# Batched transposed matmul: b as bf16 pairs four rows to a partition, next batch's transposes ahead

## Chip, cores, metric

The kernel runs on one core of one Trainium2 chip. The metric is the device time of one execution in microseconds (us), median of several; the profile's own span is 1.7 to 1.9 us shorter than that time.

Names: PE is TensorE, which multiplies and also transposes; PEld is its loading of weights; DVE is VectorE, ACT ScalarE, POOL GpSimd, and SP the queue that issues the DMAs. PSUM is the memory that PE writes to; an eviction is a copy out of it. A transfer has landed when all 16 DMA engines have done their part of it. LAG n means that the output of a batch is stored n batches later. The granted clock is a share of TensorE's full clock.

## The reference

```python
batch, m, k, n = 16, 512, 512, 512
a: (batch, k, m) float32      b: (batch, n, k) float32
out = np.matmul(a.transpose(0, 2, 1), b.transpose(0, 2, 1))     # (batch, m, n) float32
```

Each batch reads 1 MiB of a and 1 MiB of b and writes 1 MiB: 48 transfers, 50.33 MB in all. b has k along its rows, so it must be transposed on the chip before it can be multiplied.

## The kernel before

```python
a_v = a.rearrange("b (ki ko) m -> b ki ko m", ko=KO)     # partition = 4 rows in a run: 8 KB
b_v = b.rearrange("b (no ni) k -> b ni no k", ni=P)      # partition = 4 rows 128 apart: 4 x 2 KB
out_v = out.rearrange("b (mi mo) n -> b mi mo n", mo=MO) # 8 KB
...                      # pools: a and b 3 buffers, o 8; PSUM 4 + 4 banks
LAG = 6                                                  # outputs are stored six batches later
for i in range(B):
    ...                                                  # load b, load a (both on the SP queue)
    for rk in range(KO):
        nc.scalar.copy(a_bf[:, rk, :], a_sb[:, rk, :])               # L60: a to bf16
    for rk in range(KO):
        bt_ps = psum_t.tile([P, N], f32)
        for no in range(NO):                                         # L68: 16 fp32 transposes
            nc.tensor.transpose(bt_ps[:, no * P:(no + 1) * P], b_sr[:, no, rk, :], identity)
        nc.vector.tensor_copy(bt_sb[:, rk, :], bt_ps)                # L73: to bf16
    for rm in range(MO):
        ...                                                          # L80: 4 matmuls into o_ps
        if rm % 2 == 0: nc.scalar.copy(o_sb[:, rm, :], o_ps)         # L88
        else:           nc.vector.tensor_copy(o_sb[:, rm, :], o_ps)  # L90
    if i >= LAG: emit_out_dma(i - LAG)
for j in range(B - LAG, B): emit_out_dma(j)
```

## Time and profile before

| | before |
|---|---|
| time | 129.46 us (129.3 to 129.65) |
| span in the profile | 127.8 us |
| DMA queue 1 | 97.5% of 16 engines' span, 13056 packets |
| PE / DVE / ACT busy | 72% / 48% / 43% |

The first lines are from the page of the kernel before: the span in 40 equal slices (DMA busy in tenths, then GB/s), the packets, the DMA queue, and the chain of work that ended last.

```profile
DMA  3999999999999999999999999999999999999980
GB/s 90 402 370 422 406 399 420 382 409 398 404 417 415 417 419 394 416 410 429 420 410 423 406 436 405 416 426 413 427 402 431 412 424 418 426 428 428 426 346 36
DMA packets 13063, 50.42 MB, mean 394 GB/s; under 512 B 768, under 2 KB 768, under 8 KB 8960
...
q1 hardware_dynamic: 13056, 50.33, 97.5%
...
DMA 50%; PE 34%; SPq 3%; ACT 1%; issue 1%; DVE 1%; ACTq 0%
```

The DMA engines are busy in every slice but the first and the last two. The 8960 packets under 8 KB are b's 8192 packets of 2 KB and 768 small ones that signal completion; a and out are 4096 packets of 8 KB. The rate rises from about 400 to 420 GB/s as outputs mix in and holds 426 to 428 in the last full slices, which move outputs alone. That fits slower packets of b, but the row alone doesn't show it: loads of a and b are mixed in it.

The groups of instructions (busy us, mean ns of one | idle before, and what ended it), and the waits (us in total, times, longest):

```profile
L80 PE MATMUL o_ps<-bt_sb,a_bf 128*128 128x512 bf16 x248 | 59.0, 385 | 9.1 <-ACT a_bf L60 8.7
L73 DVE CAST bt_sb<-bt_ps 128x512 bf16<-128x512 f32 x64 | 40.0, 683 | 14.7 <-PE bt_ps L68 14.7
L68 PE MATMUL bt_ps<-identity,b_sb 128*128 128x128 f32 x256 | 35.7, 295 | 12.8 <-DMA b_sb<-in_b_dram 12.8
```

```profile
ACT a_bf L60 <- DMA a_sb<-in_a_dram: 39.5, 13, 6.8
```

ACT, which casts a, waits 39.5 us for a's transfers. The compute engines wait for the DMA, not the DMA for them.

The end of the span, by window: PE, PEld, DVE, ACT, POOL busy us (instructions), granted clock, DMA share, GB/s.

```profile
110.00:115.00 5.00, 3.64 (x15) 1.61 (x16) 2.12 (x4) 3.35 (x6) 0.00 (x0) 1.00 1.01 424
115.00:120.00 5.00, 0.00 (x0) 0.00 (x0) 0.10 (x1) 0.00 (x0) 0.00 (x0) 0.74 1.02 431
120.00:123.00 3.00, 0.00 (x0) 0.00 (x0) 0.00 (x0) 0.00 (x0) 0.00 (x0) 0.50 1.01 429
123.00:126.00 3.00, 0.00 (x0) 0.00 (x0) 0.00 (x0) 0.00 (x0) 0.00 (x0) 0.50 0.40 169
```

Compute is over at 115.1 us and the DMA goes on at its full rate to about 123 us: seven outputs were still to be stored when the last load came in.

### The profile page before, as it was taken

The numbers are of one execution on the slowest core, as the hardware profiler recorded it, in microseconds if no ns is written. First come the engines' busy times: TensorE is split into PE (matmuls) and PEld (weight loads), VectorE is DVE, ScalarE is ACT, GpSimd is POOL, SyncE is SP. The second block draws the span as 40 slices with busy tenths as digits, with TensorE's granted clock in tenths as the row PEclk, the third lists the DMA queues.
The fourth block names the chain that finished last, engine by engine and source line by source line (L and its number), as shares of the span: only waits on it lengthen the run. The fifth ranks groups of instructions, "written<-read, shape, count | busy, mean of one in ns | idle before, by whom it ended". The sixth has DMA issues, their size and how long they took to land.

```text
span 127.8 us, 1405 instructions
## 1 busy us (share of the span) xinstructions
PE 92.5 (72%) x504; PEld 60.6 (47%) x512; DVE 61.5 (48%) x96; ACT 54.8 (43%) x97; POOL 0.7 (1%) x6
## 2 busy tenths in 40 slices
PE   0099999999999995768767796877779777670000
PEld 0094858678586763364634536353364634430000
DVE  0053668586774865463544727355472635640000
ACT  4026747646674635407163460816337072540000
POOL 2000000000000000000000000000000000000000
PEclk9999999999999999999999999999999999998555
DMA  3999999999999999999999999999999999999980
GB/s 90 402 370 422 406 399 420 382 409 398 404 417 415 417 419 394 416 410 429 420 410 423 406 436 405 416 426 413 427 402 431 412 424 418 426 428 428 426 346 36
DMA packets 13063, 50.42 MB, mean 394 GB/s; under 512 B 768, under 2 KB 768, under 8 KB 8960
## 3 DMA queue, kind: packets, MB, share of 16 engines
q1 hardware_dynamic: 13056, 50.33, 97.5%
q8 instruction: 4, 0.07, 0.2%
q14 instruction: 3, 0.02, 0.0%
HBM read 33.55 MB, written 16.78 MB: 394 GB/s over the span
## 4 chain that ended last, share of the span: by engine, by line
DMA 50%; PE 34%; SPq 3%; ACT 1%; issue 1%; DVE 1%; ACTq 0%
DMA a_sb<-in_a_dram 32%; PE o_ps L80 22%; DMA out_dram<-o_sb 13%; PE bt_ps L68 12%; DMA b_sb<-in_b_dram 4%; SPq L56 3%; ACT a_bf L60 1%; DVE o_sb L90 1%; ACT o_sb L88 0%; ACTq L60 0%; SPq L50 0%
## 5 line engine op out<-in xcount | busy, mean ns | idle before, releaser
L80 PE MATMUL o_ps<-bt_sb,a_bf 128*128 128x512 bf16 x248 | 59.0, 385 | 9.1 <-ACT a_bf L60 8.7
L60 ACT CAST a_bf<-a_sb 128x512 bf16<-128x512 f32 x64 | 34.9, 615 | 39.6 <-DMA a_sb<-in_a_dram 39.5
L73 DVE CAST bt_sb<-bt_ps 128x512 bf16<-128x512 f32 x64 | 40.0, 683 | 14.7 <-PE bt_ps L68 14.7
L68 PE MATMUL bt_ps<-identity,b_sb 128*128 128x128 f32 x256 | 35.7, 295 | 12.8 <-DMA b_sb<-in_b_dram 12.8
L80 PEld LDWEIGHTS <-a_bf 128*128 128x128 bf16 x256 | 27.3, 115 | 35.8 <-ACT a_bf L60 17.7
L68 PEld LDWEIGHTS bt_ps<-identity,b_sb 128*128 128x128 f32 x256 | 33.9, 211 | 17.5 <-PE o_ps L80 8.5
L90 DVE COPY o_sb<-o_ps 128x512 f32<-128x512 f32 x32 | 22.1, 692 | 38.9 <-PE o_ps L80 21.9
L88 ACT COPY o_sb<-o_ps 128x512 f32<-128x512 f32 x32 | 18.8, 586 | 19.0 <-PE o_ps L80 18.9
L60 ACT ACT_TABLE_LOAD x1 | 1.3, 1283 | 0.7 <-PEq L111 0.7
masks.py:199 POOL TENSOR_SCALAR_AFFINE_SELECT identity<-identity 128x128 f32<-128x128 f32 x1 | 0.3, 292 | 0.1
masks.py:197 POOL MEMSET identity<- 128x128 f32 x1 | 0.2, 204 | 0.3 <-POOLq L111 0.3
L111 POOL MEMSET const-bfloat16-1.0<- 128x1 bf16 x1 | 0.1, 101 | 0.0
L111 POOL MEMSET const-uint8-127<- 128x1 uint8 x1 | 0.1, 101 | 0.0
L111 POOL MEMSET const-float32-0.0<- 128x1 f32 x1 | 0.1, 98 | 0.2 <-issue 0.2
L111 POOL MEMSET const-float32-1.0<- 128x1 f32 x1 | 0.1, 98 | 0.0
## 6 DMA issues: line engine op xcount, KB each, us to landing
b_sb<-in_b_dram SPq DMA_DIRECT2D x16, 1024.0 KB, 15.4
a_sb<-in_a_dram SPq DMA_DIRECT2D x16, 1024.0 KB, 17.3
out_dram<-o_sb SPq DMA_DIRECT2D x16, 1024.0 KB, 17.4
```

What stands on the lines that cost most here:

```text
L56: nc.sync.dma_start(a_sb, a_v[i])
L60: nc.scalar.copy(a_bf[:, rk, :], a_sb[:, rk, :])
L68: nc.tensor.transpose(bt_ps[:, no * P:(no + 1) * P], b_sr[:, no, rk, :], identity,)
L73: nc.vector.tensor_copy(bt_sb[:, rk, :], bt_ps)
L80: nc.tensor.matmul(o_ps, a_br[:, rk, rm, :], bt_sb[:, rk, :], start=(rk == 0), stop=(rk == KO - 1),)
L88: nc.scalar.copy(o_sb[:, rm, :], o_ps)
L90: nc.vector.tensor_copy(o_sb[:, rm, :], o_ps)
L111: nc = _bacc.Bacc("TRN2", target_bir_lowering=False, num_devices=1)
```

## The change

Four rows of b in a run go to one partition, so that b too moves in 8 KB packets; the copy out of PSUM then puts n back in order. b is cast to bf16 first and transposed as 32-bit words of two bf16 values, which halves the transposes; the matmuls read every second bf16 of the result. And the source puts the transposes of batch i ahead of the matmuls of batch i-1. Besides, outputs lag by three batches in place of six, and the buffers of a and b go from three to four.

```diff
-    b_v = b.rearrange("b (no ni) k -> b ni no k", ni=P)
+    b_v = b.rearrange("b (ni no) k -> b ni no k", no=NO)
 ...  (a_pool, b_pool 3 -> 4; ac_pool 4 -> 3; bc_pool 2 new; o_pool 8 -> 6)
-    LAG = 6
+    LAG = 3
 ...
+    def prepare(i):
+        bc = bc_pool.tile([P, NO, K], cdt, name="bc")
+        nc.vector.tensor_copy(bc, b_sb)                                  # L65
+        bc_w = bc.bitcast(f32).rearrange("p no (pk j) -> p no j pk", j=KJ)
+        bt_w = bt_sb.rearrange("p j (ni no) -> p j ni no", no=NO)
+        for j in range(KJ):
             for no in range(NO):
-                nc.tensor.transpose(bt_ps[:, no * P:(no + 1) * P], b_sr[:, no, rk, :], identity)
-            nc.vector.tensor_copy(bt_sb[:, rk, :], bt_ps)
+                nc.tensor.transpose(bt_ps[:, no, :], bc_w[:, no, j, :], identity)           # L74
+            nc.vector.tensor_copy(bt_w[:, j, :, :], bt_ps.rearrange("p no ni -> p ni no"))  # L75
+        b_use[i] = bt_sb.bitcast(cdt).rearrange("p j (n h) -> p j h n", h=2)
 ...  (a is cast in two copies of 1024 columns: L80; matmuls L89; output copies L97 ACT, L99 DVE)
+    for i in range(B + 1):
+        if i < B:
+            load(i); prepare(i)
+        if i >= 1:
+            multiply(i - 1)
+        if i >= LAG + 1:
+            nc.sync.dma_start(out_v[i - 1 - LAG], o_tiles.pop(i - 1 - LAG))
```

More of the change, by code (lines that the diff above doesn't have):

```diff
@@ L23 @@
     KO = K // P
+    KJ = KO // 2
     MO = M // P
@@ L36 @@
     make_identity(nc, identity)
-    a_pool = ctx.enter_context(tc.tile_pool(name="a_pool", bufs=3))
-    b_pool = ctx.enter_context(tc.tile_pool(name="b_pool", bufs=3))
-    ac_pool = ctx.enter_context(tc.tile_pool(name="ac_pool", bufs=4))
+    a_pool = ctx.enter_context(tc.tile_pool(name="a_pool", bufs=4))
+    b_pool = ctx.enter_context(tc.tile_pool(name="b_pool", bufs=4))
+    ac_pool = ctx.enter_context(tc.tile_pool(name="ac_pool", bufs=3))
+    bc_pool = ctx.enter_context(tc.tile_pool(name="bc_pool", bufs=2))
@@ L41 @@
     bt_pool = ctx.enter_context(tc.tile_pool(name="bt_pool", bufs=3))
-    o_pool = ctx.enter_context(tc.tile_pool(name="o_pool", bufs=8))
+    o_pool = ctx.enter_context(tc.tile_pool(name="o_pool", bufs=6))
     psum_t = ctx.enter_context(tc.tile_pool(name="psum_t", bufs=4, space=bass.MemoryType.PSUM))
     psum_o = ctx.enter_context(tc.tile_pool(name="psum_o", bufs=4, space=bass.MemoryType.PSUM))
-    LAG = 6
-    o_tiles = {}
-    def emit_out_dma(j):
-        nc.sync.dma_start(out_v[j], o_tiles.pop(j))
@@ L52, with load @@
-    for i in range(B):
-        b_sb = b_pool.tile([P, NO, K], f32)
+    LAG = 3
+    o_tiles, a_tiles, b_tiles, a_use, b_use = {}, {}, {}, {}, {}
+    def load(i):
+        b_tiles[i] = b_sb = b_pool.tile([P, NO, K], f32, name="b_sb")
         nc.sync.dma_start(b_sb, b_v[i])
-        a_sb = a_pool.tile([P, KO, M], f32)
+        a_tiles[i] = a_sb = a_pool.tile([P, KO, M], f32, name="a_sb")
         nc.sync.dma_start(a_sb, a_v[i])
-        a_bf = ac_pool.tile([P, KO, M], cdt)
-        for rk in range(KO):
-            nc.scalar.copy(a_bf[:, rk, :], a_sb[:, rk, :])
-        a_br = a_bf.rearrange("p rk (pm rm) -> p rk rm pm", rm=MO)
-        b_sr = b_sb.rearrange("p no (pk rk) -> p no rk pk", rk=KO)
-        bt_sb = bt_pool.tile([P, KO, N], cdt)
-        for rk in range(KO):
-            bt_ps = psum_t.tile([P, N], f32)
-            for no in range(NO):
-                nc.tensor.transpose(
-                    bt_ps[:, no * P:(no + 1) * P],
-                    b_sr[:, no, rk, :],
-                    identity,
-                )
-            nc.vector.tensor_copy(bt_sb[:, rk, :], bt_ps)
-        o_sb = o_pool.tile([P, MO, N], f32)
-        o_tiles[i] = o_sb
+    def prepare(i):
+        b_sb, a_sb = b_tiles.pop(i), a_tiles.pop(i)
+        bc = bc_pool.tile([P, NO, K], cdt, name="bc")
+        nc.vector.tensor_copy(bc, b_sb)
+        bc_w = bc.bitcast(f32).rearrange("p no (pk j) -> p no j pk", j=KJ)
+        bt_sb = bt_pool.tile([P, KJ, N], f32, name="bt_sb")
+        bt_w = bt_sb.rearrange("p j (ni no) -> p j ni no", no=NO)
+        for j in range(KJ):
+            bt_ps = psum_t.tile([P, NO, P], f32, name="bt_ps")
+            for no in range(NO):
+                nc.tensor.transpose(bt_ps[:, no, :], bc_w[:, no, j, :], identity)
+            nc.vector.tensor_copy(bt_w[:, j, :, :], bt_ps.rearrange("p no ni -> p ni no"))
+        b_use[i] = bt_sb.bitcast(cdt).rearrange("p j (n h) -> p j h n", h=2)
+        a_bf = ac_pool.tile([P, KO, M], cdt, name="a_bf")
+        for h in range(2):
+            nc.scalar.copy(a_bf[:, 2 * h:2 * h + 2, :], a_sb[:, 2 * h:2 * h + 2, :])
+        a_use[i] = a_bf.rearrange("p rk (pm rm) -> p rk rm pm", rm=MO)
@@ L77, with multiply @@
+    def multiply(i):
+        a_br, bt_h = a_use.pop(i), b_use.pop(i)
+        o_tiles[i] = o_sb = o_pool.tile([P, MO, N], f32, name="o_sb")
         for rm in range(MO):
-            o_ps = psum_o.tile([P, N], f32)
+            o_ps = psum_o.tile([P, N], f32, name="o_ps")
             for rk in range(KO):
@@ L82 @@
                     a_br[:, rk, rm, :],
-                    bt_sb[:, rk, :],
+                    bt_h[:, rk // 2, rk % 2, :],
                     start=(rk == 0),
@@ L90 @@
                 nc.vector.tensor_copy(o_sb[:, rm, :], o_ps)
-        if i >= LAG:
-            emit_out_dma(i - LAG)
+    for i in range(B + 1):
+        if i < B:
+            load(i)
+            prepare(i)
+        if i >= 1:
+            multiply(i - 1)
+        if i >= LAG + 1:
+            nc.sync.dma_start(out_v[i - 1 - LAG], o_tiles.pop(i - 1 - LAG))
     for j in range(B - LAG, B):
-        emit_out_dma(j)
+        nc.sync.dma_start(out_v[j], o_tiles.pop(j))
 _INS = ['a', 'b']
```

## The prediction

> **What bounds the kernel now.** The DMA engines. Queue 1 takes 97.5% of 16 engines' span (page, DMA queues), and the slices show DMA at 9 from about 3 to 122 us. It moves 50.33 MB; the issue-by-issue record keeps about 16 engines occupied from 2.8 to 122.8 us. The windows give 404-412 GB/s while only loads run (20-40 us), 416-424 once outputs mix in, 431 when only outputs remain (115-120 us). PE is 9.95 of 10 us busy only until about 45 us (5.37 us a batch); afterwards PE, DVE and ACT wait for loads (ACT for a_sb 39.5 us, PE for b_sb 12.8 us, view of waits). The chain of waits is 50% DMA.
>
> **What the change does to compute (off the critical path).** Per batch: 16 transposes become 8 (about 120 ns apart in the chain of waits: -0.96 us PE); four 0.68 us bt evictions become two fp32 ones (-1.4 us DVE), plus one DVE cast of 2048 columns. Estimate for that cast: at the rate of the 683 ns eviction it would be at most 2.3 us, probably about 1.2 from SBUF at double rate. ACT casts 4x615 ns become two of about 1.05 us (estimate). Matmuls (about 215 ns apart) now read b at a 4-byte step; the Trainium skill, "SBUF - State Buffer", section "Door 1: The DMA port swizzle", calls up to 8 bf16 of step free; no run here shows it for the moving operand yet. PE then needs about 4.4 us a batch, DVE 4-5, ACT 3.3, against 7.4 us of DMA. All this only moves waits; PE stops bounding the first 45 us, but the DMA engines had no gap there either, so that is worth nearly nothing.
>
> **What matters: b's packets.** b is read today as 8192 packets of 2 KB, a and out as 4096 of 8 KB. With four rows to a partition b also becomes 2048 packets of 8 KB. The packet records have 84 ns median (86 mean) per 2 KB and 309 (313) per 8 KB: 4x84 = 336 against 309. Packets overlap, so I fitted packets to wall time: 80-83 ns per 2 KB, 307-313 per 8 KB, or 320-332 against about 309 per 8 KB. Saving: 2048 x 11 to 23 ns / 16 engines = 1.4-2.9 us (4.4 us by raw means). The Trainium skill, "DMA: Bandwidth & Descriptors", section "Why small descriptors are slow (HBM only)", gives the mechanism: a fixed cost per packet.
>
> **The end.** With LAG 3, five outputs instead of seven follow the last load. Estimate from b15's landing: cast 1.2, transposes 1, matmuls 14 and 15 3.6 us each, eviction 0.7: output 15 is ready about 10.2 us after, when a15 and four outputs (12.3 us at 2.45) have just about been moved. A gap of 0-0.7 us. The end also has stragglers: most engines finish at 123.4-125, two at 126.7, which I blame on 16 KB instruction fetches of about 1 us; fewer instructions may save one fetch.
>
> **Prediction:** 129.5 - 2.4 - 0.5 + 0.3 = 126.9 us, 80% range 125.0 to 128.4. Faster by over 2% (below 126.87) 0.47; within 2% 0.51; slower 0.02.
>
> **What would show it.** Packets under 8 KB nearly gone; 420-430 GB/s from the first slices; PE busy falls to some 75 us; PE waits for b_sb in every batch; matmuls still 215 ns apart; the chain more than half DMA; no slice before the last two with DMA under 9.
>
> **What would make it wrong.** Packets of 8 KB mixing reads and writes running slower than 309 ns (saving gone); a fully 27 ns saving per 8 KB (about 125 us); the strided moving operand or the strided PSUM read running at half rate (PE 8 us a batch: slower than before); an output starved by in-order issue behind waits in the SP queue.

## The result and the profile after

Ratios here are the mean time of one kernel's fast runs over that of the other's of the same rounds, so they are not quite the ratio of the medians quoted beside them.

| | before | after |
|---|---|---|
| time | 129.38 us (129.2 to 129.65) | 127.58 us (127.22 to 128.23) |
| ratio | | 0.9873, 95% interval 0.9841 to 0.9905 |
| span in the profile | 127.8 us | 125.4 us |
| DMA packets of queue 1 | 13056 | 6912 |
| PE busy | 92.5 us | 85.0 us |

The time lies in the range. The page of the changed kernel, the same rows as above:

```profile
DMA  3999999999999999999999999999999999999835
GB/s 94 426 431 423 426 423 426 418 350 421 413 428 431 423 426 426 434 428 421 423 431 431 423 415 428 434 423 418 426 436 423 423 423 431 428 418 426 371 154 219
DMA packets 6918, 50.41 MB, mean 402 GB/s; under 512 B 768, under 2 KB 768, under 8 KB 768
...
q1 hardware_dynamic: 6912, 50.33, 96.1%
...
PE 47%; DMA 22%; DVE 17%; issue 7%; ACT 2%; SPq 1%; ACTq 0%
```

The 2 KB packets are gone and the rate is some 425 GB/s from the second slice on. But the last slices fall to 371, 154 and 219, and the chain that ended last is now PE and DVE, with DMA at 22%. The end, by window:

```profile
110.00:115.00 5.00, 2.99 (x15) 1.49 (x14) 2.52 (x3) 3.06 (x4) 0.00 (x0) 1.00 1.02 426
115.00:120.00 5.00, 4.67 (x24) 2.43 (x22) 1.98 (x3) 1.17 (x2) 0.00 (x0) 1.00 0.80 339
120.00:123.00 3.00, 0.00 (x0) 0.00 (x0) 0.69 (x1) 0.00 (x0) 0.00 (x0) 1.00 0.54 224
123.00:126.00 3.00, 0.00 (x0) 0.00 (x0) 0.00 (x0) 0.00 (x0) 0.00 (x0) 0.58 0.33 134
```

PE is still multiplying at 115 to 120 us, and the DMA engines run dry one after another from 118.4 us on; from 120.6 to 121.6 us all 16 are idle (packet records). The last output starts alone: it lands on all 16 engines within 0.17 us of each other, as the trace's landing records show, where the outputs before it landed over 2.3 us.

Why is PE late? The chain of waits over the last two batches (start, us, what):

```profile
105.44 0.57 issue
106.02 1.23 DVE bc L65
107.38 0.73 PE bt_ps L74 x4
108.13 0.70 DVE bt_sb L75
108.88 3.81 PE o_ps L89 x16
113.32 1.23 DVE bc L65
114.68 0.73 PE bt_ps L74 x4
115.43 0.70 DVE bt_sb L75
116.18 3.81 PE o_ps L89 x16
120.01 0.69 DVE o_sb L99
```

Cast, transposes, copy, matmuls, output copy and the next cast follow one another: one batch is 113.32 - 106.02 = 7.30 us of work in series, where the prediction had 4.4 us of PE beside 4-5 us of DVE. The order in the source is not what the chip ran. In the built program 240 matmuls, all of batches 0 to 14, stand ahead of batch 15's transposes; the source has 224 there. From batch 5 on the build had moved each batch's transposes behind all of the previous batch's matmuls, and DVE's cast of b behind the output copies of the batch before. The landing records have b of batch 15 landed at 108.64 us; its cast began at 113.32.

That order alone does not make 4.7 us, however. From batch 6 on b landed every 7.38 us, so that a chain of 7.30 us just keeps up and makes good less than 0.1 us a batch. By the landing records the cast began 0.1 us after b's landing in batch 5, then fell behind in three steps: to 2.1 us in batch 6, from 2.0 to 3.5 in batch 9, from 3.3 to 4.8 in batch 13. Before each step a batch's matmuls ran in a stretch of 3.4 us, from 38.2, 62.1 and 92.8 us, in which the granted clock was half. The chain has them beside the usual 3.81 us:

```profile
38.54 5.23 PE o_ps L89 x16
61.87 5.40 PE o_ps L89 x16
92.68 5.41 PE o_ps L89 x16
```

They lost 1.4, 1.6 and 1.6 us, 4.6 us in all (an estimate: the differences to 3.81; the first step also has 0.7 us of waiting for a). So the cast is late for two reasons together: a serial chain without slack, and the half clock that it could not make good. No run takes the half clock away alone. Over the nine fast runs of the changed kernel the four with a mean granted clock of 0.941 or 0.942 took 127.74 to 128.23 us, the five with 0.951 to 0.955 126.79 to 127.63.

The waits say the same. Of the 16 casts of b only four waited for b's transfer; nothing in steady state was early enough to wait:

```profile
DVE bc L65 <- DMA b_sb<-in_b_dram: 7.4, 4, 5.6
```

And the groups:

```profile
L89 PE MATMUL o_ps<-bt_sb,a_bf 128*128 128x512 bf16 x256 | 66.7, 414 | 5.1 <-DVE bt_sb L75 3.0
L74 PE MATMUL bt_ps<-identity,bc 128*128 128x128 f32 x128 | 19.6, 298 | 29.9 <-DVE bc L65 29.9
L75 DVE COPY bt_sb<-bt_ps 128x512 f32<-128x512 f32 x32 | 20.7, 686 | 14.6 <-PE bt_ps L74 14.6
L65 DVE CAST bc<-b_sb 128x2048 bf16<-128x2048 f32 x16 | 19.5, 1220 | 7.4 <-DMA b_sb<-in_b_dram 7.4
```

The copy that reorders n (686 ns) costs what the plain one did (683). The cast took 1220 ns; the Trainium skill, "VectorE: DVE Perf Modes", section "The perf-mode tier table (the rule you actually need)", has 1227 ns for an fp32 copy of 2048 elements in SBUF, and the trace agrees (with a bf16 output here).

### The profile page after: what moved, and what is told of

The parts are those of the page before. It is cut to its first block, busy times and chain, and to the rows that moved or that the text cites. A ratio compares the mean times of both kernels' runs of the same rounds, so it can differ in the third digit from the quotient of the medians.

```text
span 125.4 us, 1110 instructions
## 1 busy us (share of the span) xinstructions
PE 85.0 (68%) x384; PEld 45.8 (36%) x384; DVE 60.9 (49%) x80; ACT 51.3 (41%) x65; POOL 0.7 (1%) x6
## 3 DMA queue, kind: packets, MB, share of 16 engines
q1 hardware_dynamic: 6912, 50.33, 96.1%
## 4 chain that ended last, share of the span: by engine, by line
PE 47%; DMA 22%; DVE 17%; issue 7%; ACT 2%; SPq 1%; ACTq 0%
PE o_ps L89 41%; DMA a_sb<-in_a_dram 22%; DVE bc L65 10%; PE bt_ps L74 7%; DVE bt_sb L75 6%; ACT a_bf L80 2%; DVE o_sb L99 1%; SPq L55 1%; SPq L110 0%; ACTq L80 0%; SPq L57 0%
## 5 line engine op out<-in xcount | busy, mean ns | idle before, releaser
L89 PE MATMUL o_ps<-bt_sb,a_bf 128*128 128x512 bf16 x256 | 66.7, 414 | 5.1 <-DVE bt_sb L75 3.0
L89 PEld LDWEIGHTS <-a_bf 128*128 128x128 bf16 x256 | 29.6, 117 | 38.1 <-issue 12.5
L74 PE MATMUL bt_ps<-identity,bc 128*128 128x128 f32 x128 | 19.6, 298 | 29.9 <-DVE bc L65 29.9
L80 ACT CAST a_bf<-a_sb 128x1024 bf16<-128x1024 f32 x32 | 31.9, 1045 | 15.0 <-DMA a_sb<-in_a_dram 14.7
L74 PEld LDWEIGHTS bt_ps<-identity,bc 128*128 128x128 f32 x128 | 17.4, 209 | 35.6 <-issue 35.0
L75 DVE COPY bt_sb<-bt_ps 128x512 f32<-128x512 f32 x32 | 20.7, 686 | 14.6 <-PE bt_ps L74 14.6
L65 DVE CAST bc<-b_sb 128x2048 bf16<-128x2048 f32 x16 | 19.5, 1220 | 7.4 <-DMA b_sb<-in_b_dram 7.4
```

Source lines behind the costliest of these rows:

```text
L65: nc.vector.tensor_copy(bc, b_sb)
L74: nc.tensor.transpose(bt_ps[:, no, :], bc_w[:, no, j, :], identity)
L75: nc.vector.tensor_copy(bt_w[:, j, :, :], bt_ps.rearrange("p no ni -> p ni no"))
L80: nc.scalar.copy(a_bf[:, 2 * h:2 * h + 2, :], a_sb[:, 2 * h:2 * h + 2, :])
L89: nc.tensor.matmul(o_ps, a_br[:, rk, rm, :], bt_h[:, rk // 2, rk % 2, :], start=(rk == 0), stop=(rk == KO - 1),)
```

## The experiments

After the result I formed theory P, which departs from the prediction: packets worth about 4 us (as the mean packet durations have it, 4 x 86 against 309 ns), of which a gap at the end gives back some 2 to 3. Rival R1 is the prediction's own sum: packets worth 1.4 to 2.9 us. Rival R2: the gain comes from the compute engines. P1 and P2 are two reasons for the gap: compute that is late because its steps run in series (P1), or a lag of three batches that is too short by itself (P2).

| run | time, us | ratio to before | 95% interval |
|---|---|---|---|
| b_rows_only | 126.65 | 0.9795 | 0.977 to 0.9821 |
| after_old_rows | 129.48 | 1.0015 | 0.9983 to 1.0047 |
| dma_2k (no product) | 128.58 | 0.9938 | 0.9918 to 0.9958 |
| dma_8k (no product) | 125.91 | 0.9732 | 0.9715 to 0.9749 |
| after_lag6 | 126.17 | 0.9766 | 0.9739 to 0.9794 |
| after_o_on_act | 126.78 | 0.9816 | 0.9793 to 0.9839 |
| before_lag3 | 129.43 | 1.0004 | 0.9981 to 1.0026 |
| after_forced | 127.77 | 0.9861 | 0.9813 to 0.9908 |
| after_again | 127.87 | 0.9869 | 0.9834 to 0.9904 |
| lag6_again | 126.18 | 0.9769 | 0.9742 to 0.9796 |
| act_lag6 | 126.39 | 0.9773 | 0.9743 to 0.9803 |

### What are the packets worth?

**b_rows_only**: the kernel before, with b's layout alone.

```diff
-    b_v = b.rearrange("b (no ni) k -> b ni no k", ni=P)
+    b_v = b.rearrange("b (ni no) k -> b ni no k", no=NO)
-            nc.vector.tensor_copy(bt_sb[:, rk, :], bt_ps)
+            nc.vector.tensor_copy(bt_sb[:, rk, :].rearrange("p (ni no) -> p ni no", no=NO),
+                                  bt_ps.rearrange("p (no ni) -> p ni no", no=NO))
```

> The kernel before with one part of the change: b four rows to a partition (8 KB packets), n put back in order by the copy out of PSUM; transposes, order and LAG 6 stay. Theory P (packets are worth about 4 us: 16 engines x 512 packets at 84-86 ns against 128 at 309 ns, and seven outputs still cover the end): 124.7 to 125.8 us. Rival R1 (packets are worth 1.4 to 2.9 us, as predicted): 126.5 to 128 us. Rival R2 (the gain is in the halved transposes and the compute engines): 129.4 us, as before.

Measured: 126.65 us beside 129.28, 2.6 us less. This is R1's value and refutes the size in P.

**after_old_rows**: the changed kernel with b in 2 KB packets again.

```diff
-    b_v = b.rearrange("b (ni no) k -> b ni no k", no=NO)
+    b_v = b.rearrange("b (no ni) k -> b ni no k", ni=P)
```

(with the copy out of PSUM in plain order)

> The changed kernel with b's old layout (2 KB packets, no reordering in the copy). Theory P: about 4 us of packets come back, gap at the end stays 2 to 3.5 us: 130 to 132 us, slower than before. R1: 129 to 130 us. R2: 127.6 us, as the changed kernel.

Measured: 129.48 us, R1's range. Without the packets nothing of the gain is left, and no loss at the end hides one (in its profile the last output landed 2.42 us after the one before, the usual distance), so R2 falls: half the transposes, fewer instructions and the larger casts buy no time that can be measured.

**dma_2k and dma_8k**: the transfers alone, no product; the loaded a is stored as the output three batches later, a wrong result. Both have ten buffers for a and six for b, more than either kernel. They differ in b's layout alone.

```diff
-        ...  (casts, transposes, matmuls, copies)
+        if i >= LAG:
+            nc.sync.dma_start(out_v[i - LAG], a_tiles.pop(i - LAG))
```

> The transfers of the kernel before alone (b in 2 KB packets, a, and a stored as the output three batches later: wrong result on purpose, no compute). Theory P: DMA bound before, so 126.5 to 129 us.

> The same transfers alone with b four rows to a partition. Theory P: 4 to 4.5 us less than with 2 KB packets, 122.5 to 124.5 us; 309 ns a packet, reads and writes mixed. R1: 1.4 to 2.9 us less.

Measured: 128.58 and 125.91 us, 2.67 us apart. R1 again. The GB/s rows of the two pages, 2 KB packets first:

```profile
GB/s 78 406 387 418 396 403 409 429 397 405 404 426 424 387 423 406 414 420 411 427 401 434 399 416 409 419 426 405 420 414 413 418 411 423 410 420 432 424 422 106
```

```profile
GB/s 95 433 430 428 423 423 388 357 425 401 430 417 423 417 430 428 430 425 428 428 425 428 428 425 430 425 425 430 425 425 423 425 433 428 430 420 425 425 420 69
```

Two things keep P's 4 us from coming. Packet durations overstate the small packets, because these overlap: in 4 us stretches of the packet records with mostly 2 KB packets 16.5 are in flight on 16 engines, with 8 KB packets 16.1. And the 8 KB stream has a slow spell early on (388 and 357 in the seventh and eighth slice), in which 58 packets took over 350 ns, 563 in the median, in place of 309. The changed kernel has one too (350, in the ninth). What causes it stays open; it also comes without any compute, so it is not the compute engines' doing.

The transfers alone also set a floor. The kernel before is 0.6% above its own, so it was DMA bound as predicted; the changed kernel is 1.4% above its own (0.9869 to 0.9873 against 0.9732).

### What does the end cost?

**after_lag6**: the changed kernel with the old lag.

```diff
-    o_pool = ctx.enter_context(tc.tile_pool(name="o_pool", bufs=6))
+    o_pool = ctx.enter_context(tc.tile_pool(name="o_pool", bufs=9))
-    LAG = 3
+    LAG = 6
```

> The changed kernel with outputs held back six batches again (nine output buffers) and nothing else. Theory P (the changed kernel loses about 3 us in a DMA gap at its end, because the compute runs late there and only five outputs are left to move): gap gone, 124.0 to 125.2 us. R1 (no such loss beyond 0.3 us, packets small): 127.2 to 127.6 us.

Measured: 126.17 us. The loss at the end is real, which R1 as I had put it ruled out, but it is smaller than P had it. By window:

```profile
110.00:115.00 5.00, 2.52 (x12) 1.02 (x9) 1.38 (x2) 1.17 (x2) 0.00 (x0) 1.00 1.01 428
115.00:120.00 5.00, 0.00 (x0) 0.00 (x0) 0.00 (x0) 0.00 (x0) 0.00 (x0) 0.67 1.02 431
120.00:123.00 3.00, 0.00 (x0) 0.00 (x0) 0.00 (x0) 0.00 (x0) 0.00 (x0) 0.50 0.42 175
```

339 GB/s at 115 to 120 us have become 431; the compute ends before 115 us here, because an output that is stored later does not stand ahead of the loads, and the last loads come sooner.

**after_again and lag6_again** put the two in the same rounds, five of them.

> The changed kernel once more, unedited, so that it stands in the same rounds as the two below. 127.3 to 128.0 us, ratio 0.985 to 0.990 to the kernel before.

> The changed kernel with LAG 6 and nine output buffers, against the changed kernel of the same rounds. If the end costs the changed kernel what the first pair said: 126.0 to 126.4 us, 1.1 to 1.6 us below it, clear of the intervals. If the first difference came of different chips: within 0.4 us of it.

Measured: ratios 0.9869 and 0.9769, intervals clear of each other. The difference is 0.01 x 129.34 = 1.3 us: what the end costs the changed kernel. The single runs of the changed kernel spread from 126.79 to 128.03 us, those of LAG 6 from 126.11 to 126.58: with a compute chain at its end, the time also follows what happens to the chain.

**before_lag3**: is LAG 3 too short by itself?

```diff
-    LAG = 6
+    LAG = 3
```

(and six output buffers)

> The kernel before with outputs held back three batches (six buffers) in place of six. Theory P1 (LAG 3 hurts only where compute runs late; before, output 15 was ready 5.2 us after the last load landed, with 12 us of outputs to move): 129 to 130 us, no gap. Rival P2 (LAG 3 is too short by itself): 131.5 to 133 us.

Measured: 129.43 us, ratio 1.0004. LAG 3 costs the kernel before nothing. "No gap" was wrong, though:

```profile
115.00:120.00 5.00, 4.05 (x25) 2.78 (x26) 2.49 (x4) 2.35 (x5) 0.00 (x0) 1.00 1.00 421
120.00:123.00 3.00, 1.52 (x8) 0.56 (x5) 1.38 (x2) 1.01 (x2) 0.00 (x0) 1.00 0.53 221
123.00:126.00 3.00, 0.00 (x0) 0.00 (x0) 0.00 (x0) 0.00 (x0) 0.00 (x0) 1.00 0.87 360
```

There is one at 120 to 123 us, and it is free. The landing records explain why: the slowest of the 16 engines ends each of the last transfers 3.6 us behind the fastest (3.3 us in the kernel before), and it landed the last two outputs 2.41 us apart, without a pause. A gap in which the others wait for it does not move the end. I also had the number of outputs wrong in that expectation: this loop leaves four after the last load, not the 12 us that I wrote.

### Why is the compute late?

**after_o_on_act**: all output copies on ACT, so that DVE's next cast need not stand behind them.

```diff
-            if rm % 2 == 0:
-                nc.scalar.copy(o_sb[:, rm, :], o_ps)
-            else:
-                nc.vector.tensor_copy(o_sb[:, rm, :], o_ps)
+            nc.scalar.copy(o_sb[:, rm, :], o_ps)
```

> The changed kernel with all four output evictions on ACT, so that DVE's cast of the next b does not stand behind the evictions of this batch's product. LAG 3 stays. Theory P1 (the compute is late because cast, transposes, eviction, matmuls and output eviction of a batch run one after the other, 7.3 us a batch, against 7.36 us of DMA): repeat falls to under 6 us, compute keeps up with the loads, the gap at the end is under 1 us, 124.3 to 125.5 us. Rival P2 (late for another reason: LAG 3 alone is too short even for compute that keeps up): 127 to 127.8 us.

Measured: 126.78 us. It lies between P1's range (to 125.5, which rested on P's 4 us for the packets) and P2's (127 to 127.8). The mechanism is as P1 said: now 14 of 16 casts wait for the transfer of b, in place of four.

```profile
DVE bc L65 <- DMA b_sb<-in_b_dram: 48.4, 14, 5.6
```

b of batch 15 landed at 109.00 us and its cast began at 109.09, not 4.7 us later. The gap shrinks (392 GB/s at 115 to 120 us against 339) but stays, as the last batch's matmuls ran in a stretch of half clock in this profile (5.42 us for 3.82). In this profile what is left of it costs nothing: the last output landed 2.42 us after the one before, as outputs do. The chain now has slack: another stretch of half clock, at 68.5 us (5.42 us of matmuls), left the next cast 0.09 us behind b's landing. So the serial chain is shown as a cause of the late compute, and in the mean about half of the loss goes with it (0.9816 lies between 0.9869 and 0.9769; its interval touches those of both). This profiled run took 126.26 us, as LAG 6 does; the other three took 126.69 to 127.02, and where their loss lies is open.

**after_forced**: the order that the source has, held by explicit order edges.

```diff
+    # first matmul of batch i: a dependency, without a semaphore, on the last transpose of batch i + 1
+    if rm == 0 and rk == 0 and i + 1 in last_t:
+        _behind(tc, mm, last_t[i + 1])
```

> The changed kernel with the order that its source has, held by explicit order edges: the transposes of batch i+1 ahead of all matmuls of batch i (the built program of the changed kernel has them behind). LAG 3. If the intended order takes the cast and transposes out of the serial 7.3 us, compute keeps up with the loads and output 15 is ready about 10.2 us after the last b lands, the sum in the prediction: 124.5 to 125.7 us. If the order makes no odds: 127.6 us.

Measured: 127.77 us, ratio 0.9861: no better than the changed kernel. The intended order is thus worth nothing here that these runs can tell. The end of its profile:

```profile
112.91 7.45 PE L95 MATMUL o_ps<-bt_sb,a_bf 128*128 128x512 bf16 x31
```

Both last batches are multiplied in a row, after the last b has come (it landed at 109.34 us). The order ties output 14 to the load of b 15 as well, so that two outputs are late in place of one (of the two only the last landed late, 3.42 us after the one before); the window from 115 to 120 us has 280 GB/s, less than the changed kernel's 339. A rival stands beside this: a stretch of half clock from 104.8 us (batch 13's matmuls 5.39 us for 3.80) held b 15's cast 1.2 us behind its landing, where the two casts before had been 0.1 us behind. The runs do not separate the two.

**act_lag6**: both mends.

> Both mends together, LAG 6 and all output evictions on ACT. With no gap left at the end, compute that keeps up has nothing more to give: the same as LAG 6 alone within 0.3 us, near the 125.9 us of the transfers alone. If late compute still costs something with LAG 6: 0.3 to 0.8 us less than LAG 6 alone.

Measured: 126.39 us, ratio 0.9773 against 0.9769 for LAG 6 alone: the same. Where outputs cover the end, late compute costs nothing. This and LAG 6 alone are the fastest kernels that compute the product, some 2.3% faster than before and within half a percent of the transfers alone. b_rows_only, the kernel before with three lines changed, is at 0.9795, and its interval overlaps theirs.

## Why the prediction was right or wrong

The time was right: 126.9 predicted with 125.0 to 128.4, 127.6 to 127.9 measured; "within 2%" had 0.51 and came true, with "faster" at 0.47, so that this part was little more than a coin's toss. The 126.9 itself was 0.7 to 1 us too low.

- **DMA bound before**: right. The transfers alone take 128.58 us of 129.48.
- **Packets, 2.4 us**: right. 2.6 us (b_rows_only) and 2.67 us (transfers alone). Fitting packets to wall time was the right reading; the raw means (4.4 us, offered as the upper case, and taken up by theory P after the result) were too high.
- **Compute off the critical path**: right for all but the end. after_old_rows is as slow as before.
- **The end, "a gap of 0-0.7 us", + 0.3 us in the sum**: this is the term that was mis-sized. It measured 1.3 us. The step that failed is "output 15 is ready about 10.2 us after": it took 12.1 us (b landed at 108.64, the last copy ended at 120.70). The sum took the order from the source, in which nothing but b's landing holds the cast. On the chip the cast of b 15 waited 4.7 us more for the previous batch's output copies, while matmuls that the sum put after the cast were done before it. The sum also had the full clock throughout; three stretches of half clock had put the serial chain behind by about that much. The second half of the failure is that the sum let an output move as soon as it was ready. Output 15 was issued at 120.76 us, just after the last packet of output 14 had ended (120.59, landed at 121.00), and its first packets started at 121.59. It landed 3.61 us after output 14, where outputs land 2.43 us apart: 1.2 us lost in this profile, which agrees with the 1.3 us.
- **Stragglers, -0.5 us for fewer instruction fetches**: not shown. LAG 6 (three 16 KB fetches) against b_rows_only (four) differ by 0.29% in ratio in the same rounds, inside the intervals, and in more than the fetches. That a fetch sets an engine back is supported: in the profile of after_lag6 all engines land within 0.26 us of each other until a 16 KB fetch at 31.0 us, and the next transfer to land, at 34.2 us, has 1.55 us. But the transfers alone, which fetch nothing, drift to 2.1 us as well, in the slow spells. So fetches are probably one cause of two; no run changes them alone.
- **"matmuls still 215 ns apart"**: wrong by a little, off the path. 216 ns in the median before and in b_rows_only, 227 ns in the changed kernel and in the other two with the 4-byte step that I looked at (after_old_rows, LAG 6).
- **"PE waits for b_sb in every batch"**: wrong. It waited for the cast, which waited for b in four batches.
- **The other signs**: no packets of 2 KB left, and 420 to 430 GB/s from the first slices (426, 431, 423): right. PE busy some 75 us: wrong, 85.0. The chain more than half DMA: wrong, 22%. No slice before the last two with DMA under 9: wrong, the third from the end has 8.

The sum with the measured terms: 129.4 - 2.6 (packets) - 0.3 (rest: LAG 6 against b_rows_only, not resolved) + 1.3 (end) = 127.8 us.

## What to carry to other kernels

In a kernel that the DMA bounds, packet size is worth what the wall clock per packet says, not what packet durations say; measure it with the transfers alone, which also gives the floor. Read the order of instructions from the built program or the trace before you sum up the end of a kernel: a build may undo the order of the source, and an engine that works in program order then ties unrelated work together, as DVE did here with the cast and the output copies. A chain that only just keeps up with the loads (7.30 against 7.38 us) can't make good a delay. Keep enough outputs in hand to cover the last batch's whole chain; that mends a late end more surely than making the chain shorter.

## What the Trainium skill lacked or had wrong

- "SBUF - State Buffer", section "Door 1: The DMA port swizzle (why `[64,N]` ≈ `[32,N]`)": it calls a step of up to 8 bf16 free. Matmuls whose moving operand steps by two bf16 started 227 ns apart in the median, those with contiguous bf16 216 ns (three kernels with the step, two without). The step was not changed alone, so this does not show the page wrong.
- "DMA: Bandwidth & Descriptors", section "Why small descriptors are slow (HBM only)": it gives the mechanism, a fixed cost per packet, and the runs agree in direction. It has no figure for 2 KB against 8 KB in a mixed stream: 2.67 us on 50.33 MB, of which a third changed size, and the durations of single packets (84 against 309 ns) overstate it because small packets overlap.
- No page that I read has by how much the engines drift apart within a full queue, or what that does to a gap at the end: late in a run the slowest of 16 engines landed 2.0 to 3.6 us after the fastest, and the drift grew at 16 KB instruction fetches and in slow spells and was not made up while the queue was full. A gap at the end shorter than that cost nothing (before_lag3).
- "TensorE: Matmul & The Clock Gate", section "What's actually happening": its window of 3413 ns agrees with the stretches of half clock in the changed kernel, 3.4 us each at 38, 62 and 93 us. The advice under "Why this matters for your kernels" to avoid idle gaps over about 3 us is not enough to keep the clock: the profile has 2.0 to 2.8 us without PE work ahead of most batches' transposes, and a stretch with a batch's matmuls at half clock (5.2 to 5.4 against 3.8 us) came three times after such gaps. The kernel before, which waits twice in shorter pieces, kept the full clock until its compute ended.
